# A two-product GELU kernel: another order for the opening loads and transposes, for the second block of b and for the late turns of a

## The chip, the cores and the metric

The kernel runs on one core of one Trainium2 chip. Times are device microseconds of one execution, lower is better. Profile times are microseconds from the start of the span unless marked ns.

## The reference

With a of 1024 x 1024, b of 1024 x 2048 and c of 2048 x 1024, all float32:

```python
h = np.matmul(a, b)
h = 0.5 * h * (1 + np.tanh(np.sqrt(2 / np.pi) * (h + 0.044715 * h ** 3)))
return np.matmul(h, c).astype(np.float32)
```

## The kernel before

The program is written with its order by hand: each engine executes its instructions in the order in which the kernel's lines issue them. PE is TensorE, DVE is VectorE, ACT is ScalarE, POOL is GpSimd, and SP is the queue that issues most loads and stores. POOL issues the loads that turn float32 into bf16 on the way.

The first product is made transposed: a block of 128 columns of b is the stationary operand, and 512 rows of a, transposed and in bf16, are the moving one. One result is therefore a tile of 128 columns of h by 512 rows, summed over eight slices of 128 along the contraction. There are 16 such tiles (t = 0 to 15) for each half of a's rows. ACT applies the GELU as it takes a tile out of PSUM. The transposes of a are made by PE, and DVE copies them out of PSUM.

The first half of a's rows goes in three stages:

- **Block one**, t = 0 to 5 (L102 for the products). SP loads a in five column groups across all four row tiles (L76, pieces of 512 or 1024 bytes) and eight slices of b, 768 columns wide (L82), alternately. For each slice k, DVE casts a's four blocks (L107), PE transposes them (L110), DVE copies them out (L111), ACT casts the slice of b in two halves (L113), and PE then multiplies the slice before. Ten products of zeros (L96) occupy PE at the head.
- **Block two**, t = 6 to 9 (L134). POOL loads its columns of b in four DMAs of two slices each (L126). The loop takes the slices outermost, so all four result tiles grow together in four PSUM buffers.
- **Tiles t = 10 to 15** (L143, in `mm1`), each of which takes all eight slices by itself. POOL loads their columns of b (`b_hi`) in four DMAs, and then the second half of a's rows in four DMAs of one row tile each (L155). `turn(j)` transposes one of these row tiles by eight transposes (L162) and one DVE copy (L163). The turns stand after t = 11, 12, 13 and 14.

POOL's loads of b start when a small copy on POOL, the gate (L91), has seen slice 5 of block one's b arrive. After the four turns the second half of a's rows goes through all 16 tiles.

The second product is a 2 x 2 block scheme with seven block products (L242), whose sums and differences of blocks DVE makes (L196 to L235). The sums of c begin when the second half-column of c has been loaded into the buffer that the transposed first half of a used. The last output tile is made in two pieces of 256 columns, each added (L312) and stored by itself.

PSUM is split into two pools: `ppool` with six buffers, and `tpool` with two, which the transposes use.

Of the kernel before, what the change touches and what calls it, by code (L numbers as in the profile page):

```python
# [9 lines left out]
F32 = mybir.dt.float32  # L10
BF16 = mybir.dt.bfloat16
F32R = mybir.dt.float32r
SUB = mybir.AluOpType.subtract
ADD = mybir.AluOpType.add
AF = mybir.ActivationFunctionType
# [4 lines left out]
def kernel(ctx, tc, a, b, c, out):  # L20
    nc = tc.nc
    M, K = a.shape
    _, N = b.shape
    _, P = c.shape
    KT = K // 128
    NT = N // 128
    MT = M // 128
    H = 512
    N0 = 6
    W0 = N0 * 128  # L30
    N1 = 4
    W1 = N1 * 128

    av = a.rearrange("(mt p) k -> p mt k", p=128)
# [6 lines left out]
    astage = ctx.enter_context(tc.tile_pool(name="astage", bufs=4))  # L41
    abf = ctx.enter_context(tc.tile_pool(name="abf", bufs=4))
# [3 lines left out]
    tpool = ctx.enter_context(tc.tile_pool(name="tpool", bufs=2, space=PSUM))  # L46

    warm = consts.tile([128, H], BF16, name="warm")
    nc.vector.memset(warm, 0.0)
    ident = consts.tile([128, 128], BF16, name="ident")  # L50
# [3 lines left out]
    aT = [keep.tile([128, KT, H], BF16, name=f"aT{h}", tag=f"A{h}") for h in range(2)]  # L54
    WB = W0 + W1
    b_lo = keep.tile([128, KT, WB], BF16, name="b_lo", tag="B0")
    b_hi = keep.tile([128, KT, N - WB], BF16, name="b_hi", tag="B1")

    def bcols(k0, kn, n0, w):
        if n0 < WB:  # L60
            return b_lo[:, k0:k0 + kn, ds(n0, w)]
        return b_hi[:, k0:k0 + kn, ds(n0 - WB, w)]

    def bt(k, t):
        return bcols(k, 1, t * 128, 128)[:, 0, :]
# [5 lines left out]

    a_st, b_st = {}, {}

    def load_a0(k, n):
        st = astage.tile([128, 4, 256], F32, name="a_st")
        nc.sync.dma_start(out=st[:, :, 0:n * 128], in_=av[:, 0:4, ds(k * 128, n * 128)])  # L76
        for i in range(n):
            a_st[k + i] = st[:, :, ts(i, 128)]

    def load_b0(k):  # L80
        st = b0stage.tile([128, W0], F32, name="b0_st")
        nc.sync.dma_start(out=st, in_=bv[:, k, 0:W0])  # L82
        b_st[k] = st

    gate = consts.tile([128, 1], F32, name="gate")
    for k, n in ((0, 1), (1, 1), (2, 2), (4, 2), (6, 2)):
        load_a0(k, n)
        for i in range(n):
            load_b0(k + i)

    nc.gpsimd.tensor_copy(gate, b_st[5][:, 0:1])  # L91
    g = consts.tile([128, 1], F32, name="g")
    nc.scalar.activation(g, warm[:, 0:1], AF.Gelu_apprx_tanh)
    wps = tpool.tile([128, H], F32, name="pt")
    for _ in range(10):
        nc.tensor.matmul(wps, warm[:, 0:128], warm, start=True, stop=True)  # L96

    ps = [ppool.tile([128, H], F32, name="ps") for _ in range(N0)]

    def mm0(k):  # L100
        for t in range(N0):
            nc.tensor.matmul(ps[t], bt(k, t), aT[0][:, k, :],  # L102
                             start=(k == 0), stop=(k == KT - 1))

    for k in range(KT):
        ab = abf.tile([128, 4, 128], BF16, name="ab")
        nc.vector.tensor_copy(ab, a_st[k])  # L107
        pt = tpool.tile([128, H], BF16, name="pt")
        for j in range(4):
            nc.tensor.transpose(pt[:, ts(j, 128)], ab[:, j, :], ident)  # L110
        nc.vector.tensor_copy(aT[0][:, k, :], pt)  # L111
        for i in range(2):
            nc.scalar.activation(b_lo[:, k, ts(i, W0 // 2)], b_st[k][:, ts(i, W0 // 2)], AF.Copy)  # L113
        if k > 0:
            mm0(k - 1)
    mm0(KT - 1)

    def gelu(t, h, p):
        nc.scalar.activation(hq[h][t // NH][:, t % NH, :], p, AF.Gelu_apprx_tanh)  # L119
# [5 lines left out]
    def load_b(k0, kn, n0, w):  # L125
        nc.gpsimd.dma_start(out=bcols(k0, kn, n0, w), in_=bv[:, k0:k0 + kn, ds(n0, w)])  # L126

    ps = [(tpool if t < 2 else ppool).tile([128, H], F32, name="pt" if t < 2 else "ps")
          for t in range(N1)]
    for k in range(0, KT, 2):  # L130
        load_b(k, 2, W0, W1)
        for i in range(2):
            for t in range(N1):
                nc.tensor.matmul(ps[t], bt(k + i, N0 + t), aT[0][:, k + i, :],  # L134
                                 start=(k + i == 0), stop=(k + i == KT - 1))
# [4 lines left out]
    def mm1(t, h):  # L140
        p = ppool.tile([128, H], F32, name="ps")
        for k in range(KT):
            nc.tensor.matmul(p, bt(k, t), aT[h][:, k, :],  # L143
                             start=(k == 0), stop=(k == KT - 1))
        gelu(t, h, p)
# [7 lines left out]
    for j in range(4):  # L153
        st = abf.tile([128, K], BF16, name="ab1")
# [3 lines left out]
    def turn(j):  # L158
        ab = a1[j]
        pt = tpool.tile([128, KT, 128], BF16, name="pt")  # L160
        for k in range(KT):
            nc.tensor.transpose(pt[:, k, :], ab[:, ts(k, 128)], ident)  # L162
        nc.vector.tensor_copy(aT[1][:, :, ts(j, 128)], pt)  # L163

    for t in range(N0 + N1, NT):
        mm1(t, 0)
        if NT - 5 <= t < NT - 1:
            turn(t - (NT - 5))

# [6 lines left out]
    c21 = keep.tile([128, NH, H], BF16, name="c21")  # L178
# [25 lines left out]
    for t in range(NT):  # L204
# [10 lines left out]
        if WB // 128 <= t < WB // 128 + 4:  # L215
            i = t - WB // 128
# [20 lines left out]
    def bank(w=H):  # L237
        return ppool.tile([128, w], F32, name="ps", padded_shape=[128, H])

    def prod(p, lhs, rhs, j, q=slice(0, H)):  # L240
        for t in range(NH):
            nc.tensor.matmul(p, lhs(t)[:, ts(j, 128)], rhs(t)[:, q],  # L242
                             start=(t == 0), stop=(t == NH - 1))

    def whole(x):
        return lambda t: x[:, t, :]
# [10 lines left out]
    def new_out():  # L257
        return opool.tile([128, H], F32, name="ot")

    def store(ot, m, q0, w=H):  # L260
        nc.sync.dma_start(out=out[ts(m, 128), ds(q0, w)], in_=ot[:, 0:w])

    def combine(m, q, p, u, op=ADD, swap=False):
        ot = new_out()
        nc.vector.tensor_tensor(ot, u if swap else p, p if swap else u, op=op)  # L265
        store(ot, m, q * H)
# [5 lines left out]
    for j in R:  # L272
        p = bank()
        prod(p, whole(h11), whole(c11), j)
        nc.scalar.activation(u2[j], p, AF.Copy)  # L275
    for j in range(3):
        p = bank()
# [3 lines left out]
    last_keep = opool.tile([128, H], F32, name="lk", bufs=1)  # L281
    nc.gpsimd.tensor_copy(last_keep, last)  # L282
    for j in R:
        p = bank()
        prod(p, halves(s2), ones(t2), j)
        nc.vector.tensor_tensor(u2[j], p, u2[j], op=ADD)
    for j in R:
        p = bank()
# [3 lines left out]
    for j in R:  # L292
        p = bank()
# [5 lines left out]
    for j in R:  # L299
        p = bank()  # L300
        prod(p, halves(s2), whole(c22), j)
        combine(j, 1, p, u2[j])
    for j in R:
        p = bank()
        prod(p, whole(h22), ones(t2), j)
        combine(4 + j, 0, p, u3[:, j, :], op=SUB, swap=True)
    for q in range(2):
        w = H // 2
        p = bank(w)
        prod(p, whole(h12), whole(c21), 3, q=ds(q * w, w))  # L310
        ot = new_out()
        nc.vector.tensor_tensor(ot[:, 0:w], p, last_keep[:, ds(q * w, w)], op=ADD)  # L312
        store(ot, 3, q * w, w)

# [1 line left out]
_INS = ['a', 'b', 'c']  # L316
# [26 lines left out]
```

## Time and profile before

| | |
|---|---|
| median of 13 runs | 126.71 us (125.42 to 127.51) |
| the profiled execution | 125.42 us, of which the span is 123.6 |
| PE | 114.5 us busy, 93% of the span |
| DVE | 65.2 us, 53% |
| ACT | 29.6 us, 24% |
| DMA | 18.43 MB written at their targets, 20.97 MB read from HBM |

A line of the timeline gives start, length, engine, source line, operation, operands and count, and in brackets the idle time just before it and what ended that. Matmuls are pipelined, so the starts of successive ones tell more than their lengths. A DMA's landing time is its issue's start plus its time to landing.

### The profile page before, as it was taken

How to read it: one execution, taken by the hardware profiler on the slowest of the kernel's cores; microseconds unless marked ns; L12 is line 12 of the kernel's file. 1: busy time of each engine (PE TensorE's matmuls, PEld its weight loads, DVE VectorE, ACT ScalarE, POOL GpSimd, SP SyncE). 2: the span in 40 equal slices, each digit the busy share in tenths (PEclk: the TensorE clock that was granted, in tenths of full speed). 3: DMA queues.
4: the chain of work that ended last, by engine and by line, in shares of the span. 5: the costliest groups of instructions: out<-in, count | busy, mean ns of one | idle time of the engine just before them, and what ended most of it. 6: DMA issues, size and time to landing. Idle time of an engine off the chain costs nothing.

```text
span 123.6 us, 1446 instructions
## 1 busy us (share of the span) xinstructions
PE 114.5 (93%) x562; PEld 66.9 (54%) x562; DVE 65.2 (53%) x94; ACT 29.6 (24%) x54; POOL 22.2 (18%) x28
## 2 busy tenths in 40 slices
PE   6947899999599999999999999999999999999990
PEld 2323344444255544444444444468888888888860
DVE  0134451000042200007999999999569999964440
ACT  4144456707211332333223332100000000000000
POOL 2000099433440130000000000895000000000000
PEclk9999999999999999999999999999999999999999
DMA  3799999999999999995000000001500022444433
GB/s 100 172 386 377 380 325 182 194 201 203 212 205 207 329 393 225 206 206 88 0 3 0 5 0 0 0 0 60 194 0 0 5 85 99 155 184 155 170 139 115
DMA packets 14245, 18.43 MB, mean 149 GB/s; under 512 B 800, under 2 KB 9760, under 8 KB 14240
## 3 DMA queue, kind: packets, MB, share of 16 engines
q0 software_dynamic: 8000, 8.91, 39.2%
q1 hardware_dynamic: 6240, 9.44, 21.6%
q8 instruction: 4, 0.07, 0.2%
q14 instruction: 1, 0.01, 0.0%
HBM read 20.97 MB, written 4.19 MB: 204 GB/s over the span
## 4 chain that ended last, share of the span: by engine, by line
PE 70%; DMA 17%; POOL 5%; SPq 4%; issue 0%; DVE 0%
PE ps L242 41%; PE ps L143 28%; DMA ab<-in_a_dram 10%; DMA b_st<-in_b_dram 7%; SPq L82 3%; POOL b_hi L126 2%; POOL b_lo L126 2%; SPq L76 2%; PE pt L162 2%; DVE ot L312 0%; POOL gate L91 0%
## 5 line engine op out<-in xcount | busy, mean ns | idle before, releaser
L119 ACT ACTIVATE h<-ps 128x512 fp32r<-128x512 f32 (+1 forms) x30 | 17.3, 601 | 28.6 <-PE ps L143 27.4
L143 PE MATMUL ps<-aT,b_hi 128*128 128x512 bf16 x96 | 21.7, 379 | 0.0
L143 PE MATMUL ps<-aT,b_lo 128*128 128x512 bf16 x80 | 17.4, 379 | 0.0
L242 PE MATMUL ps<-t,s 128*128 128x512 f32 x64 | 15.1, 393 | 0.0
L143 PEld LDWEIGHTS <-b_hi 128*128 128x128 bf16 x96 | 9.2, 98 | 10.4
L242 PE MATMUL ps<-t,h 128*128 128x512 f32 x64 | 14.8, 389 | 0.0
L242 PE MATMUL ps<-c,h 128*128 128x512 bf16 (+1 forms) x72 | 14.2, 356 | 0.0
L242 PEld LDWEIGHTS ps<-t,s 128*128 128x128 f32 x64 | 12.0, 188 | 2.6
L242 PEld LDWEIGHTS ps<-t,h 128*128 128x128 f32 x64 | 12.0, 188 | 2.5
L282 POOL COPY lk<-u 128x512 f32<-128x512 f32 x1 | 7.3, 7312 | 33.4 <-ACT u L275 33.4
L143 PEld LDWEIGHTS <-b_lo 128*128 128x128 bf16 x80 | 7.8, 98 | 9.5
L163 DVE COPY aT<-pt 128x1024 bf16<-128x1024 bf16 x4 | 2.8, 692 | 19.0 <-PE pt L162 19.0
L196 DVE TENSOR_TENSOR t<-c,c 128x1024 fp32r<-128x1024 bf16 x4 | 4.7, 1222 | 15.1 <-DMA c<-in_c_dram 14.9
L102 PE MATMUL ps<-aT,b_lo 128*128 128x512 bf16 x48 | 11.5, 379 | 0.0
L242 PEld LDWEIGHTS <-h 128*128 128x128 bf16 x72 | 7.0, 98 | 7.0 <-issue 0.3
L113 ACT ACTIVATE b_lo<-b_st 128x384 bf16<-128x384 f32 x16 | 7.5, 515 | 9.9 <-DMA b_st<-in_b_dram 9.8
L184 POOL DMA_DIRECT2D c<-in_c_dram x8 | 6.0, 745 | 13.1 <-PE ps L143 6.9
L265 DVE TENSOR_TENSOR ot<-ps,u 128x512 f32<-128x512 f32 x11 | 7.3, 683 | 1.1 <-PE ps L242 1.1
L242 PE MATMUL ps<-c,s 128*128 128x512 f32 x32 | 7.4, 389 | 0.0
L242 PEld LDWEIGHTS ps<-c,s 128*128 128x128 f32 x32 | 6.0, 188 | 1.2
L111 DVE COPY aT<-pt 128x512 bf16<-128x512 bf16 x8 | 3.4, 425 | 6.2 <-PE pt L110 6.2
L102 PEld LDWEIGHTS <-b_lo 128*128 128x128 bf16 x48 | 4.4, 98 | 4.0
(37 smaller groups left out, 92.6 us busy)
## 6 DMA issues: line engine op xcount, KB each, us to landing
out_dram<-ot SPq DMA_DIRECT2D x15, 256.0 KB, 2.1
b_st<-in_b_dram SPq DMA_DIRECT2D x8, 384.0 KB, 8.4
c<-in_c_dram POOLq DMA_DIRECT2D x6, 512.0 KB, 14.5
c<-in_c_dram POOLq DMA_DIRECT2D x2, 1024.0 KB, 15.4
a_st<-in_a_dram SPq DMA_DIRECT2D x3, 512.0 KB, 8.8
b_hi<-in_b_dram POOLq DMA_DIRECT2D x4, 384.0 KB, 9.9
b_lo<-in_b_dram POOLq DMA_DIRECT2D x4, 256.0 KB, 5.8
ab<-in_a_dram POOLq DMA_DIRECT2D x4, 256.0 KB, 12.7
```

What stands on the lines that cost most here:

```text
L82: nc.sync.dma_start(out=st, in_=bv[:, k, 0:W0])
L102: nc.tensor.matmul(ps[t], bt(k, t), aT[0][:, k, :], start=(k == 0), stop=(k == KT - 1))
L111: nc.vector.tensor_copy(aT[0][:, k, :], pt)
L113: nc.scalar.activation(b_lo[:, k, ts(i, W0 // 2)], b_st[k][:, ts(i, W0 // 2)], AF.Copy)
L119: nc.scalar.activation(hq[h][t // NH][:, t % NH, :], p, AF.Gelu_apprx_tanh)
L126: nc.gpsimd.dma_start(out=bcols(k0, kn, n0, w), in_=bv[:, k0:k0 + kn, ds(n0, w)])
L143: nc.tensor.matmul(p, bt(k, t), aT[h][:, k, :], start=(k == 0), stop=(k == KT - 1))
L184: nc.gpsimd.dma_start(out=dst[:, t:t + 4, :], in_=cv[:, r * NH + t:r * NH + t + 4, ts(q, H)])
L196: nc.vector.tensor_tensor(t1[i], c12[:, ts(i, 2), :], c11[:, ts(i, 2), :], op=SUB)
L242: nc.tensor.matmul(p, lhs(t)[:, ts(j, 128)], rhs(t)[:, q], start=(t == 0), stop=(t == NH - 1))
L265: nc.vector.tensor_tensor(ot, u if swap else p, p if swap else u, op=op)
L282: nc.gpsimd.tensor_copy(last_keep, last)
```

## The change

Four places are altered.

1. The opening. SP loads a by row tiles: tiles 0 and 1 in whole rows, tiles 2 and 3 as two half rows each, with the first two slices of b between the halves. The casts and transposes go by row tile and half row (four 128 x 128 blocks): `half` casts on DVE or on ACT, `turn0` transposes and copies out on DVE or on ACT. Six of the eight groups of transposes stand ahead of block one, and the second halves of tiles 2 and 3 inside its slices 1 and 2. Each slice of b is cast half on DVE and half on ACT. The products of zeros are eight at the head and three after the second and the fourth group; they write into the last of block one's PSUM buffers. The gate waits for slice 4 of b.
2. Block two's part of b comes in two DMAs of four slices.
3. The turns of the second half of a stand after t = 13 (one) and t = 14 (three).
4. The last output tile is cut into 384 and 128 columns.

```diff
-    def load_a0(k, n):
-        st = astage.tile([128, 4, 256], F32, name="a_st")
-        nc.sync.dma_start(out=st[:, :, 0:n * 128], in_=av[:, 0:4, ds(k * 128, n * 128)])
-        for i in range(n):
-            a_st[k + i] = st[:, :, ts(i, 128)]
+    def load_a0(mt, k0, n):
+        st = astage.tile([128, n * 128], F32, name="a_st")
+        nc.sync.dma_start(out=st, in_=av[:, mt, ds(k0 * 128, n * 128)])
+        a_st[mt, k0] = st
...
-    for k, n in ((0, 1), (1, 1), (2, 2), (4, 2), (6, 2)):
-        load_a0(k, n)
-        for i in range(n):
-            load_b0(k + i)
-
-    nc.gpsimd.tensor_copy(gate, b_st[5][:, 0:1])
+    load_a0(0, 0, KT)
+    load_a0(1, 0, KT)
+    load_a0(2, 0, 4)
+    load_a0(3, 0, 4)
+    load_b0(0)
+    load_b0(1)
+    load_a0(2, 4, 4)
+    load_a0(3, 4, 4)
+    for k in range(2, KT):
+        load_b0(k)
+
+    nc.gpsimd.tensor_copy(gate, b_st[4][:, 0:1])
...
-    wps = tpool.tile([128, H], F32, name="pt")
-    for _ in range(10):
-        nc.tensor.matmul(wps, warm[:, 0:128], warm, start=True, stop=True)
-
     ps = [ppool.tile([128, H], F32, name="ps") for _ in range(N0)]
 
-    def mm0(k):
+    def warm_up(n):
+        for _ in range(n):
+            nc.tensor.matmul(ps[N0 - 1], warm[:, 0:128], warm, start=True, stop=True)
+
+    warm_up(8)
+
+    def half(mt, k0, off=0):
+        src = a_st[mt, k0 - off][:, ds(off * 128, 512)]
+        ab = abf.tile([128, 512], BF16, name="ab")
+        if off or mt == 3:
+            nc.scalar.activation(ab, src, AF.Copy)
+        else:
+            nc.vector.tensor_copy(ab, src)
+        return ab
+
+    def turn0(mt, k0, ab):
+        pt = tpool.tile([128, 4, 128], BF16, name="pt")
+        for k in range(4):
+            nc.tensor.transpose(pt[:, k, :], ab[:, ts(k, 128)], ident)
+        dst = aT[0][:, k0:k0 + 4, ts(mt, 128)]
+        if k0 == 0 and mt != 2:
+            nc.vector.tensor_copy(dst, pt)
+        else:
+            nc.scalar.activation(dst, pt, AF.Copy)
+
+    HW = W0 // 2
+
+    def cast_b0(k):
+        nc.vector.tensor_copy(b_lo[:, k, 0:HW], b_st[k][:, 0:HW])
+        nc.scalar.activation(b_lo[:, k, HW:W0], b_st[k][:, HW:W0], AF.Copy)
+
+    steps = [(0, 0, 0), (0, 4, 4), (1, 0, 0), (1, 4, 4), (2, 0, 0), (3, 0, 0)]
+    ab = [half(*x) for x in steps[:2]]
+    for i, x in enumerate(steps):
+        if i % 2 == 0 and i + 2 < len(steps):
+            ab += [half(*y) for y in steps[i + 2:i + 4]]
+        turn0(x[0], x[1], ab[i])
+        if i in (1, 3):
+            warm_up(3)
+    cast_b0(0)
+    cast_b0(1)
+    for k in range(KT):
+        if k == 1:
+            ab = [half(2, 4), half(3, 4)]
+        if k > 0 and k + 1 < KT:
+            cast_b0(k + 1)
         for t in range(N0):
             nc.tensor.matmul(ps[t], bt(k, t), aT[0][:, k, :],
                              start=(k == 0), stop=(k == KT - 1))
+            if k in (1, 2) and t == 2:
+                turn0(k + 1, 4, ab[k - 1])
...
-    for k in range(0, KT, 2):
-        load_b(k, 2, W0, W1)
-        for i in range(2):
+    for k in range(0, KT, 4):
+        load_b(k, 4, W0, W1)
+        for i in range(4):
...
-        if NT - 5 <= t < NT - 1:
-            turn(t - (NT - 5))
+        if t == NT - 3:
+            turn(0)
+        if t == NT - 2:
+            turn(1)
+            turn(2)
+            turn(3)
...
-    for q in range(2):
-        w = H // 2
+    for q0, w in ((0, 384), (384, 128)):
         p = bank(w)
-        prod(p, whole(h12), whole(c21), 3, q=ds(q * w, w))
+        prod(p, whole(h12), whole(c21), 3, q=ds(q0, w))
```

The loop over the slices that stood here before (cast, four transposes, copy, two casts of b, products of the slice before) is taken out; it is in the kernel's code above.

More of the change, by code (lines that the diff above doesn't have):

```diff
@@ L103, in mm0 @@
                              start=(k == 0), stop=(k == KT - 1))
[L105 to L111, printed above, removed]
-        for i in range(2):
[L113 to L116, printed above, removed]
+            if k in (1, 2) and t == 2:
+                turn0(k + 1, 4, ab[k - 1])
     def gelu(t, h, p):
@@ L129 @@
           for t in range(N1)]
-    for k in range(0, KT, 2):
-        load_b(k, 2, W0, W1)
-        for i in range(2):
+    for k in range(0, KT, 4):
+        load_b(k, 4, W0, W1)
+        for i in range(4):
             for t in range(N1):
@@ L306 @@
         combine(4 + j, 0, p, u3[:, j, :], op=SUB, swap=True)
-    for q in range(2):
-        w = H // 2
+    for q0, w in ((0, 384), (384, 128)):
         p = bank(w)
-        prod(p, whole(h12), whole(c21), 3, q=ds(q * w, w))
+        prod(p, whole(h12), whole(c21), 3, q=ds(q0, w))
         ot = new_out()
-        nc.vector.tensor_tensor(ot[:, 0:w], p, last_keep[:, ds(q * w, w)], op=ADD)
-        store(ot, 3, q * w, w)
+        nc.vector.tensor_tensor(ot[:, 0:w], p, last_keep[:, ds(q0, w)], op=ADD)
+        store(ot, 3, q0, w)
 _INS = ['a', 'b', 'c']
```

## The prediction

> **What bounds the kernel now.** I read the page's busy shares first: PE 93% of 123.6 us, so only PE's gaps can be won. The PE timeline says where they are (start, length, engine and line, operation, count, idle before it and its releaser):
>
> ```profile
> 1.19 4.45 PE L96 MATMUL pt<-warm 128*128 128x512 bf16 x10 [1.19 <-DVE warm L49]
> 5.43 0.58 PE L110 MATMUL pt<-ident,ab 128*128 128x128 bf16 x4
> 7.84 0.40 PE L110 MATMUL pt<-ident,ab 128*128 128x128 bf16 x4 [1.82 <-DVE ab L107]
> 8.07 1.46 PE L102 MATMUL ps<-aT,b_lo 128*128 128x512 bf16 x6
> ...
> 19.09 2.75 PE L102 MATMUL ps<-aT,b_lo 128*128 128x512 bf16 x12
> 21.68 0.59 PE L134 MATMUL pt<-aT,b_lo 128*128 128x512 bf16 x2
> ...
> 28.58 3.62 PE L143 MATMUL ps<-aT,b_hi 128*128 128x512 bf16 x16
> 33.64 0.62 PE L162 MATMUL pt<-ident,ab 128*128 128x128 bf16 x8 [1.44 <-DMA ab<-in_a_dram]
> 34.10 1.89 PE L143 MATMUL ps<-aT,b_hi 128*128 128x512 bf16 x8
> ```
>
> The opening (block one, 48 products of L102) runs from 8.07 to 21.68, though twelve products take 21.68 - 19.09 = 2.59, or 0.216 each, so that 48 need 10.4. Block two (32 of L134) follows to 28.58 without a gap. Then one wait of 1.44 to 1.6 us, before the first turn (L162) at 33.64. The chain of waits confirms it, and shows nothing but PE after it:
>
> ```profile
> 21.37 12.22 DMA ab<-in_a_dram
> 33.59 0.05 issue
> 33.64 0.62 PE pt L162 x8
> ...
> 40.78 29.35 PE ps L143 x136
> 70.14 50.17 PE ps L242 x232
> ```
>
> The stage table (stretch, length, busy time of PE, PEld, DVE, ACT and POOL, clock, DMA share, GB/s) tells what feeds the opening:
>
> ```profile
> 3.00:4.00 1.00, 1.00 (x4) 0.33 (x3) 0.43 (x1) 0.00 (x0) 0.00 (x0) 1.00 1.13 221
> 4.00:5.00 1.00, 1.00 (x3) 0.30 (x2) 0.00 (x0) 0.00 (x0) 0.00 (x0) 1.00 0.54 124
> 5.00:6.00 1.00, 1.00 (x6) 0.52 (x4) 0.00 (x0) 0.13 (x1) 0.00 (x0) 1.00 0.47 140
> 6.00:7.00 1.00, 0.01 (x1) 0.00 (x0) 0.42 (x1) 0.81 (x2) 0.00 (x0) 1.00 1.10 387
> ```
>
> DMA is full from 6 us on at 370 to 390 GB/s, with a hole of about 1 us between 4 and 6. The same 5.24 MB are loaded after the change, so bytes in order decide.
>
> **What the Trainium skill says.** "DMA: Bandwidth & Descriptors", Queues, rings and completion order: an SDMA engine drains one queue's ring in order and alternates between queues. The trace agrees: a queue's landings come in issue order. "TensorE: Matmul & The Clock Gate", Part 1: the array starts at half clock and is released after a window of about 3.4 us of activity, which runs free of the kernel. The trace agrees: the ten warm-ups take 0.445 each, later products 0.216; four transposes take 0.58 at 5.43 and 0.40 at 7.84. "ScalarE: Activation LUTs", What ACT_TABLE_LOAD costs: an ACTIVATE is 186 ns + 0.833 per element, 612 for 512; the gelu row shows 594 to 606, and L113's 384 elements take 515 where the formula gives 506.
>
> **The change, part by part.**
>
> *1. Loads and start of block one.* SP issues 14 loads instead of 13 (0.43 to 0.5 each), a first. The first product now needs a's tiles 0, 1 and the halves of 2 and 3 (1.57 MB) and b's slice 0, and the next products slice 1: 2.36 MB. Before, issue plus time to landing in the tile view gives b slice 2 at 3.26 + 7.5 = 10.8 with 2.23 MB ahead of and in it, slice 3 at 3.81 + 8.0 = 11.8 with 2.62 MB. Interpolated, 2.36 MB is in at 11.1, and 1.57 MB (between slice 1, 1.31 MB at 8.3, and the third load of a, 1.84 MB at 9.8) at 9.05. The old order began with 0.52 MB of 512-byte packets; rows of 2 to 4 KB should be quicker. I take 0.45 off (estimate, between 0 and the hole's 1.0 more): halves of a at 8.6, slice 1 at 10.7. The two late halves of a wait on SP for a staging buffer, that is for the casts of tiles 0 and 1, with slices 2 to 7 behind them; the latter casts end near 8, when 0.8 MB or more is still queued, over 2 us, so DMA does not run dry.
>
> From 8.6 ACT has a cast (0.61), two copies from PSUM (0.61 each) and half a slice's cast (0.515): 10.95. DVE waits for the last transpose, which needs a PSUM buffer freed by ACT at 9.85: transposes 0.35, copy 0.43 (L111: 425 ns), half a slice 0.36 (from L107, 443 for 512): 11.0. Block one starts at **10.9** (9.7 to 11.7) instead of 8.07. It is then PE alone: 48 x 0.216 + two groups of four transposes at 0.23 = 10.8, end **21.75** instead of 21.68. Its casts keep up: slice k is due at 10.9 + 1.3k, and lands every 1.04 us (0.39 MB) from 10.7. The 24 other transposes (24 x 0.057 = 1.4) and the 6 added warm-ups (6 x 0.216 = 1.3) lie between 5 and 10.9, while PE waits for a; without that cover they would cost up to 2.7. ACT's total in the opening goes from 16 x 0.515 = 8.2 to 8 x 0.515 + 9 x 0.61 = 9.6, DVE's from 6.9 to about 5.9, both under 21.
>
> *2. Block two in two DMAs.* POOL issues 2 x 0.75 less, so the four b_hi loads and a's second half are queued 1.5 us earlier, behind full DMA engines: nothing won, and nothing lost, since POOL has only DMA issues until 77. The first product of block two now waits for four slices (1.05 MB read) rather than two. Before, the second of four loads landed at 16.2 + 5.5 = 21.7; the gate (slice 4 instead of 5) opens at 15.3 to 15.0 and less lies ahead, so 21.3 to 21.7, against PE at 21.75. I take 0, bounds 0 and 0.6; a win is excluded, since PE has no gap here now. The second half is due 3.45 later, at 25.2, where the last of the four landed at 24.35.
>
> *3. Late turns.* From block two's end E + 6.91 PE does four tiles (8 x 0.216 = 1.73 each), one turn (0.445), a tile, three turns, a tile. The first turn is due at 21.75 + 6.9 + 6.9 = 35.6; its tile landed at 33.6: the wait of 1.6 goes. The other three are due from 37.7; the last landed at 24.66 + 12.7 = 37.4. New: three turns in a row have two PSUM buffers, so the third waits for the first one's copy (L163, 0.69): 0.5. That copy pair at the end is hidden by the last tile's 1.73. Sum from the end of block one: 6.91 + 6 x 1.73 + 4 x 0.445 + 0.5 = 19.55, where it was 42.34 - 21.68 = 20.65 (1.6 of it waiting).
>
> *4. The end.* Two pieces of 256 columns become 384 and 128. PE: 8 x 0.16 + 8 x 0.057 (L162's pace) = 1.74 against 16 x 0.107 = 1.71. The last DVE addition shrinks from 0.42 to about 0.3, but waits for the bigger one before it (0.55). SP: two stores as before (0.33 each). I take 0, bounds -0.2 and +0.2.
>
> *Sum:* 21.75 + 19.55 = 41.3 against 42.34: **1.05 us** won. What follows must move up too:
>
> ```profile
> 56.40 2.36 DVE L196 TENSOR_TENSOR t<-c,c 128x1024 fp32r<-128x1024 bf16 x2 [14.89 <-DMA c<-in_c_dram]
> ...
> 75.41 4.62 DVE L226 TENSOR_TENSOR s<-s,h 128x1024 fp32r<-128x1024 f32 x4
> ...
> 87.74 0.69 DVE L286 TENSOR_TENSOR u<-ps,u 128x512 f32<-128x512 f32 x1 [0.18 <-PE ps L242]
> 89.63 0.69 DVE L286 TENSOR_TENSOR u<-ps,u 128x512 f32<-128x512 f32 x1 [1.19 <-PE ps L242]
> ```
>
> DVE waits for c at 56.4, which a full DMA brings no sooner, and is then behind until 87.7. Its sums s2 are done at 80.0, PE wants them at 81.9: 1.85 us of slack, so 1.05 passes through and little over 1.9 would.
>
> The profiled execution took 125.42 (span 123.6 and 1.8 around it), the lowest of 13 with median 126.71. 125.42 - 1.05 = 124.37, 0.992 of it; on the median, **125.7**.
>
> **Rivals.**
> *Hole gone.* The 1 us hole may belong to the 512-byte packets and the hop between tensors. Then loads come 1 us earlier, block one starts near 9.7, and 1.9 is won before the s2 slack is used up: 124.8. Against it: the first 512-byte packets moved 281 GB/s before the hole, so it may lie in the memory and stay.
> *Late start eats it.* No packet gain, or a link more in the ACT and DVE chain: block one at 11.7, end 22.5, 0.3 won: 126.4. For it: ACT carries four 0.6 us steps in series just there.
> *Half clock (slower).* Before, ten warm-ups in one piece made PE busy from 1.19 to 5.64. Now eight end near 4.6, and bursts of 0.4 to 1.3 us with gaps up to 2 us follow until 10.9. If the activity window falls badly, block one begins at 0.427 per product. A window of 3.4 us costs 1.7, the 4.2 us or more seen at the start (1.19 to past 5.43) 2.1; from 2.1 us at half speed on the gain is gone. That gives 127.4 to 127.8. For it: the window is free; against it: before, gaps of 1.8 with single transposes between them did no harm.
> That the late turns do not do what they say, because a's second half lands late again, would give back up to 1.6 and falls under the second rival.
>
> **How the numbers follow.** 0.50 for the forecast (its own range 125.0 to 126.05), 0.15 hole gone, 0.17 late start, 0.18 half clock. 0.5% is 0.63 us, about what a measurement here can tell from no change. Faster 0.50 + 0.15 = 0.65, same 0.17, slower 0.18. The range takes in the hole's case with its bounds below and most of half clock: 124.0 to 127.6.
>
> **What would show it.** First L148 product at 10.9 and 48 of them without a wait; block two within 0.6 after; no wait of a turn for DMA, but 0.5 before the fourth; start of the second half's tiles at 41.3; everything after it 1.05 earlier, with no PE wait at s2. Wrong if products of block one are spaced 0.427, if ACT or DVE casts hold PE inside it, if the hole has another length, or if the first s2 product waits for DVE.

## The result and the profile after

| | before | after |
|---|---|---|
| median of all runs | 126.93 us (48) | 124.01 us (11) |
| lowest to highest | 125.36 to 129.16 | 123.53 to 125.58 |
| profiled execution (span) | 125.42 (123.6) | 123.99 (122.2) |

The ratio of after to before is 0.982, with a 95% interval of 0.979 to 0.986: faster by 1.8%, some 2.3 us. The two profiled executions differ by only 1.43 us. The ratio compares fast executions alone (up to 1.5% above the fastest of their kernel), so it lies nearer 1 than the quotient of the medians does. Each execution has a recorded mean TensorE clock; "at full clock" below means that it is 0.99 or more.

The PE timeline of the changed kernel (start, length, engine and line, operation, count, idle before it and its releaser):

```profile
1.19 3.60 PE L103 MATMUL ps<-warm 128*128 128x512 bf16 x8 [1.19 <-DVE warm L49]
...
7.64 0.39 PE L119 MATMUL pt<-ident,ab 128*128 128x128 bf16 x4
8.49 0.38 PE L119 MATMUL pt<-ident,ab 128*128 128x128 bf16 x4 [0.46 <-ACT aT L124]
9.66 2.26 PE L148 MATMUL ps<-aT,b_lo 128*128 128x512 bf16 x9 [0.79 <-DVE b_lo L129]
11.91 0.40 PE L119 MATMUL pt<-ident,ab 128*128 128x128 bf16 x4
12.14 0.81 PE L148 MATMUL ps<-aT,b_lo 128*128 128x512 bf16 x3
13.42 0.82 PE L148 MATMUL ps<-aT,b_lo 128*128 128x512 bf16 x3 [0.47 <-DVE b_lo L129]
...
14.30 7.29 PE L148 MATMUL ps<-aT,b_lo 128*128 128x512 bf16 x33
21.43 0.59 PE L169 MATMUL pt<-aT,b_lo 128*128 128x512 bf16 x2
...
28.33 7.07 PE L178 MATMUL ps<-aT,b_hi 128*128 128x512 bf16 x32
35.24 0.61 PE L197 MATMUL pt<-ident,ab 128*128 128x128 bf16 x8
35.69 1.89 PE L178 MATMUL ps<-aT,b_hi 128*128 128x512 bf16 x8
37.41 1.06 PE L197 MATMUL pt<-ident,ab 128*128 128x128 bf16 x16
38.80 0.61 PE L197 MATMUL pt<-ident,ab 128*128 128x128 bf16 x8 [0.33 <-DVE aT L198]
39.25 1.89 PE L178 MATMUL ps<-aT,b_hi 128*128 128x512 bf16 x8
40.97 5.34 PE L178 MATMUL ps<-aT,b_lo 128*128 128x512 bf16 x24
```

Block one (L148) now runs from 9.66 to 21.43, where it ran from 8.07 to 21.68. The wait of a turn for DMA is gone; in its place stands the 0.33 us before the fourth turn. The second half of a's rows starts at 40.97 instead of 42.34, and that 1.37 us reaches the end whole. The chain of waits says the same: after block one it has PE and one 0.7 us copy, and ahead of that the loads of b's slice 2.

```profile
6.40 6.58 DMA b_st<-in_b_dram
...
13.42 0.82 PE ps L148 x3
...
38.06 0.70 DVE aT L198
...
39.41 29.35 PE ps L178 x136
68.76 49.71 PE ps L281 x224
```

The stage table of the opening (stretch, length, busy time of PE, PEld, DVE, ACT and POOL, clock, DMA share, GB/s):

```profile
3.00:4.00 1.00, 1.00 (x4) 0.33 (x3) 0.00 (x0) 0.00 (x0) 0.00 (x0) 1.00 1.00 389
4.00:5.00 1.00, 1.00 (x6) 0.38 (x5) 0.43 (x1) 0.63 (x1) 0.00 (x0) 1.00 1.01 350
...
8.00:10.00 2.00, 0.76 (x7) 0.52 (x7) 0.69 (x2) 1.42 (x3) 0.00 (x0) 1.00 0.85 245
10.00:12.00 2.00, 2.00 (x11) 0.60 (x9) 0.79 (x2) 0.52 (x1) 0.00 (x0) 1.00 1.04 409
```

The hole at 4 to 6 us is gone, and a slow stretch stands at 8 to 10, when slices 0 and 1 of b arrive.

### The profile page after: what moved, and what is told of

Its sections match the earlier page's. It is cut to its first block, busy times and chain, and to the rows that moved or that the text cites. A ratio compares the mean times of both kernels' runs of the same rounds, so it can differ in the third digit from the quotient of the medians.

```text
span 122.2 us, 1452 instructions
## 1 busy us (share of the span) xinstructions
PE 115.7 (95%) x566; PEld 67.3 (55%) x566; DVE 64.0 (52%) x93; ACT 31.2 (26%) x55; POOL 21.9 (18%) x26
## 4 chain that ended last, share of the span: by engine, by line
PE 85%; DMA 9%; DVE 1%; issue 1%; SPq 1%; ACT 1%; DVEq 0%
PE ps L281 41%; PE ps L178 31%; PE ps L148 7%; DMA b_st<-in_b_dram 5%; DMA a_st<-in_a_dram 3%; PE ps L169 3%; PE pt L169 3%; PE pt L197 1%; SPq L76 1%; DVE aT L198 1%; ACT ab L111 1%; DVE b_lo L129 0%; DVEq L376 0%; PE pt L119 0%; DVE ot L350 0%
## 5 line engine op out<-in xcount | busy, mean ns | idle before, releaser
L178 PEld LDWEIGHTS <-b_hi 128*128 128x128 bf16 x96 | 9.3, 98 | 10.8
L281 PE MATMUL ps<-c,h 128*128 128x512 bf16 (+2 forms) x72 | 14.2, 355 | 0.0
L321 POOL COPY lk<-u 128x512 f32<-128x512 f32 x1 | 8.1, 8083 | 33.2 <-ACT u L314 33.2
L148 PE MATMUL ps<-aT,b_lo 128*128 128x512 bf16 x48 | 11.2, 380 | 1.3 <-DVE b_lo L129 1.3
L148 PEld LDWEIGHTS <-b_lo 128*128 128x128 bf16 x48 | 4.4, 98 | 6.9 <-DVE b_lo L129 2.4
L103 PE MATMUL ps<-warm 128*128 128x512 bf16 x14 | 5.7, 560 | 1.2 <-DVE warm L49 1.2
L129 DVE CAST b_lo<-b_st 128x384 bf16<-128x384 f32 x8 | 3.0, 369 | 5.2 <-DMA b_st<-in_b_dram 5.2
```

Source lines behind the costliest of these rows:

```text
L103: nc.tensor.matmul(ps[N0 - 1], warm[:, 0:128], warm, start=True, stop=True)
L129: nc.vector.tensor_copy(b_lo[:, k, 0:HW], b_st[k][:, 0:HW])
L148: nc.tensor.matmul(ps[t], bt(k, t), aT[0][:, k, :], start=(k == 0), stop=(k == KT - 1))
L178: nc.tensor.matmul(p, bt(k, t), aT[h][:, k, :], start=(k == 0), stop=(k == KT - 1))
L281: nc.tensor.matmul(p, lhs(t)[:, ts(j, 128)], rhs(t)[:, q], start=(t == 0), stop=(t == NH - 1))
```

## The experiments

The ratios are to the kernel before, each on the chip of its own batch.

| run | what it is | median us | ratio, 95% interval |
|---|---|---|---|
| e1 | before, late turns alone | 124.54 | 0.987 (0.981 to 0.993) |
| e2 | before, opening alone | 126.19 | 0.996 (0.992 to 0.999) |
| e3 | before, two DMAs for block two alone | 125.82 | 0.997 (0.994 to 0.999) |
| e4 | the changed kernel, same chip | 124.77 | 0.985 (0.979 to 0.990) |

The kernel before had a median of 127.12 there. The first theory (A) gave the gain to the late turns, the rival (B) to the opening.

### e1: the late turns alone

```diff
-        if NT - 5 <= t < NT - 1:
-            turn(t - (NT - 5))
+        if t == NT - 3:
+            turn(0)
+        if t == NT - 2:
+            turn(1)
+            turn(2)
+            turn(3)
```

> The kernel before with the late turns alone. Theory A (the gain is the wait for a's second half, 1.6 us, less 0.5 for the third and fourth turn sharing two PSUM buffers): block one still starts near 8.1 and ends near 21.7, the second half's tiles start at block one's end + 19.55 (before 20.65), so 1.1 us faster than before. Theory B (the opening carries the gain, the wait would have moved or come back elsewhere): at most 0.3 us faster, with a new wait of a turn for DMA.

It is 1.7 us faster, most of the whole gain, so A holds against B; but it is more than the 1.1 that A gave. In its profile the second half starts 41.48 - 21.93 = 19.55 after the end of block one, just as A has it. Its PE timeline (the lines before the last) and POOL timeline (last line) show where the rest can come from:

```profile
28.83 7.07 PE L143 MATMUL ps<-aT,b_hi 128*128 128x512 bf16 x31
35.74 0.61 PE L162 MATMUL pt<-ident,ab 128*128 128x128 bf16 x8
...
39.30 0.61 PE L162 MATMUL pt<-ident,ab 128*128 128x128 bf16 x8 [0.34 <-DVE aT L163]
...
41.48 3.83 PE L143 MATMUL ps<-aT,b_lo 128*128 128x512 bf16 x17
...
34.78 0.74 POOL L188 DMA_DIRECT2D c<-in_c_dram x1 [0.52 <-DMA ab<-in_a_dram]
```

POOL's fifth load of c waits for the first tile of a's second half, and so dates its landing. It is released at 34.78 here, 0.9 us later than in the profiled execution of before (33.88). The turn does not notice, since it is due at 35.74. In the old place it would have cost 0.9 us more (an estimate: 34.78 - 33.88).

### e2: the opening alone

Loads, casts, transposes, warm-ups and gate of the changed kernel, everything after it as before.

> The kernel before with the new opening alone (loads, casts, transposes, warm-ups and gate); four DMAs of two slices for block two, turns after t = 11 to 14, equal end pieces. Theory A: block one ends up to 0.3 us earlier, and the wait at the first turn grows by as much, since a's second half lands at 33.3 to 33.6 as before: within 0.3 us of before. Theory B: 1 us or more faster than before, because the loads as a whole (and with them a's second half) come sooner.

It is 0.5 us faster (0.1 to 1.0), between A and B, and neither is shown by it. Block one ended some 0.5 us sooner, and the wait at the first turn grew from 1.44 to 2.16:

```profile
28.08 3.62 PE L178 MATMUL ps<-aT,b_hi 128*128 128x512 bf16 x16
33.86 0.62 PE L197 MATMUL pt<-ident,ab 128*128 128x128 bf16 x8 [2.16 <-DMA ab<-in_a_dram]
```

The first turn's tile decides when this wait ends, not PE. What is won probably comes from that landing. The load of c that it releases goes out at 34.10 here, and at 33.1 to 34.0 in seven other profiles with the new loads (the changed kernel, e4, e6, e7, e9, e11 and e12). With the old loads it goes out at 34.59 to 35.10 in e1, e3, e5 and e8, and at 33.88 in the profile of the kernel before. So the new loads probably bring a's second half some 0.5 to 1.0 us sooner than is usual before.

### e3: block two's part of b in two DMAs, alone

```diff
-    for k in range(0, KT, 2):
-        load_b(k, 2, W0, W1)
-        for i in range(2):
+    for k in range(0, KT, 4):
+        load_b(k, 4, W0, W1)
+        for i in range(4):
```

> The kernel before with block two's part of b in two DMAs of four slices, nothing else. Theory A: the first product of block two waits 0 to 0.6 us for four slices that land at 21.4 to 21.9 instead of two; the turn's wait for a takes that back, so within 0.3 us of before. Theory B's rival for this part (fewer DMAs bring a's second half earlier): a's first tile lands 0.7 us or more before 33.6 and the kernel is as much faster.

The wait came, 0.24 us before block two, and it was 0.4 us faster all the same (0.1 to 0.8), just over A's 0.3. a's first tile did not land sooner: the release of c is at 34.59. Why the change gains at all is not settled. None of its 20 executions has a mean clock of 0.973, against 13 of 41 of the kernel before on the same chip, though its first turn still waits 1.64 us.

### e4: the changed kernel on the same chip, and the clock

> The changed kernel again, on the same chip as the three parts. Theory A: 1.4 us faster than before where the granted clock is full in both, and the sum of the three parts' gains is within 0.4 of it. If the 2.2 us of the medians is real and not from slower chips among the runs of before, it shows here too, and the runs of before must have a cost that its profiled execution does not have (a longer turn wait, or a clock below 1.0 at the start).

It is 1.9 us faster at the ratio, and the three parts sum to 2.7 us. Opening and turns act on the same wait, so they may overlap; the intervals of the runs are too wide to show it. The profiled execution took 125.32 and is the half-clock rival of the prediction. Its stage table (the clock is the third column from the right), and the PE timeline's line of block one's start:

```profile
7.70:11.10 3.40, 1.63 (x12) 1.01 (x13) 1.03 (x4) 2.12 (x5) 0.00 (x0) 0.99 0.93 296
11.10:14.50 3.40, 3.18 (x11) 1.49 (x11) 1.23 (x4) 2.13 (x5) 0.00 (x0) 0.51 1.04 416
14.50:17.90 3.40, 3.40 (x20) 1.69 (x19) 1.35 (x4) 2.45 (x6) 2.53 (x4) 1.00 0.93 287
```

```profile
10.24 3.30 PE L148 MATMUL ps<-aT,b_lo 128*128 128x512 bf16 x9 [0.79 <-DVE b_lo L129]
```

PE was busy for 1.63 of 3.40 us, with no gap over 0.8, and the next 3.4 us ran at half clock: nine products in 3.30 instead of 2.12 to 2.26. The second half starts at 42.28, 1.3 us later than at full clock. Over three batches 7 of 24 executions of the changed kernel have a mean clock of 0.985 or 0.986, and take 125.2 to 125.8; the other 17 take 123.5 to 124.9.

### e5 and e8: what the wait before the first turn does to the clock

The kernel before has 78 executions in all batches with a recorded clock. 37 are at full clock (125.2 to 127.5, median 126.4), and 20 at 0.973, two stretches of half clock, with 127.6 to 129.1. Theory C laid the second stretch to the wait before the first turn; theory D to the opening or to DMA. One run filled the wait with work, another lengthened it:

```diff
+        if t == NT - 5:
+            wz = ppool.tile([128, H], F32, name="ps")
+            for _ in range(6):
+                nc.tensor.matmul(wz, warm[:, 0:128], warm, start=True, stop=True)
         if NT - 5 <= t < NT - 1:
             turn(t - (NT - 5))
```

> The kernel before with six more products of zeros just ahead of its first turn (6 x 0.216 = 1.3 us of PE work inside the wait of 1.4 to 1.6 us); turns, loads and all else as before. Theory C (the wait before the first turn costs twice: itself, and in about half of the executions a stretch of TensorE at half clock after it): the full-clock executions stay at 125.4 to 126.5, the executions at 127.5 to 129 with mean clock 0.973 go, and the median falls by 0.8 to 1.5 us. Theory D (the spread of the kernel before comes from its opening or from DMA, and the wait is only a wait): median and spread as before, or 0.1 to 0.3 us slower.

```diff
-        if NT - 5 <= t < NT - 1:
-            turn(t - (NT - 5))
+        if NT - 6 <= t < NT - 2:
+            turn(t - (NT - 6))
```

> The kernel before with its turns one tile earlier (after t = 10 to 13), so that PE waits some 3.3 us instead of 1.5 for a's second half; the tile that stood before the wait now comes after it. Theory C: the clock column falls to about 0.5 for 3.4 us or more after the wait, and the execution is 1.7 us (the moved tile) plus 1.7 us or more slower than before: 128.8 to 130.5. Theory D: clock stays 1.0 and it is 1.7 us slower, 127.1 to 127.6.

e8 took 129.68. Its PE timeline, and its stage table around the wait:

```profile
34.48 0.76 PE L162 MATMUL pt<-ident,ab 128*128 128x128 bf16 x8 [3.86 <-DMA ab<-in_a_dram]
35.03 3.48 PE L143 MATMUL ps<-aT,b_hi 128*128 128x512 bf16 x8
38.35 0.61 PE L162 MATMUL pt<-ident,ab 128*128 128x128 bf16 x8
```

```profile
31.50:34.90 3.40, 0.42 (x7) 0.42 (x8) 0.00 (x0) 0.00 (x0) 1.66 (x3) 0.99 1.16 209
34.90:38.30 3.40, 3.40 (x12) 1.34 (x10) 0.69 (x1) 0.00 (x0) 1.30 (x2) 0.51 1.16 207
```

After the wait the clock is 0.51 for 3.4 us, and eight products take 3.48 us instead of 1.89: the wait is paid twice. The clock row of e8's page (40 slices of 3.2 us, tenths of full speed) shows this stretch and an earlier one in the opening:

```profile
PEclk9967999999959999999999999999999999999998
```

Two such stretches make 0.973 of a mean (2 x 3.4 x 0.5 of 126). In e5 none of 14 executions is at 0.973 (4 of 19 of the kernel before on that chip), and the highest is 127.51. Its median fell by 0.45, less than C's 0.8; by the ratio nothing is won (0.9995, 0.996 to 1.004), since the wait for DMA itself stays.

So e8 shows C for a wait of 3.86 us. That the wait of some 1.5 us does it in the kernel before is likely and not shown: no execution of it at 0.973 was profiled, e3 has none at 0.973 with the wait in place, and e1 has one of six (and two at 0.981 and 0.982) with the wait gone.

The recorded clock also misses something. The profile of e5 has a mean clock of 1.0, and yet its first twelve products of block one are some 0.42 apart, as at half clock. Up to there e5 does not differ from the kernel before. The PE timeline, and a stretch of the stage table:

```profile
8.40 2.77 PE L102 MATMUL ps<-aT,b_lo 128*128 128x512 bf16 x6
10.96 0.63 PE L110 MATMUL pt<-ident,ab 128*128 128x128 bf16 x4
11.39 2.70 PE L102 MATMUL ps<-aT,b_lo 128*128 128x512 bf16 x6
```

```profile
8.40:10.90 2.50, 2.50 (x8) 0.91 (x7) 0.85 (x2) 0.94 (x2) 0.00 (x0) 1.00 1.05 395
```

Block one ends at 22.81 there instead of 21.68. Counts of half clock by this record are therefore lower bounds: an execution "at full clock" can have a slow opening.

### e6: the opening's gaps filled

```diff
         if i in (1, 3):
             warm_up(3)
+        if i == 4:
+            warm_up(2)
+        if i == 5:
+            warm_up(4)
```

> The changed kernel with six more products of zeros in the gaps of its opening: two after the fifth group of transposes and four after the sixth. Theory C (the changed kernel's slower executions, clock 0.986, are half clock at the start of block one, because PE was less than half busy in the window before): no execution at 0.986 with 125.2 to 125.7, all within 123.5 to 124.5. Theory D (the 0.986 has another cause): a third of the executions stay at 125.2 to 125.7. If the added products delay the transposes, 0.1 to 0.3 us slower throughout.

All six executions have a mean clock of 0.996 or more; five take 123.65 to 124.36, and one 125.74. With e11, which has the same products, that is none of 12 at 0.986, against 7 of 24 of the changed kernel. But one execution of each (125.74 and 125.21) is as slow as those at 0.986 are, and what slowed them is not known. So it is likely, and not shown, that filling the gaps rids the kernel of the executions of 125.2 and more. The ratio (0.983, 0.977 to 0.990) is no better than the changed kernel's.

### e7, e9 and e10: the slow stretch at 8 to 10 us

e7 loads the late halves of a into a buffer of their own:

```diff
-    load_a0(2, 4, 4)
-    load_a0(3, 4, 4)
+    load_late(2)
+    load_late(3)
```

> The changed kernel with the two late halves of a loaded into a buffer of their own, so that SP does not wait with them and with slices 2 to 7 of b for the casts of tiles 0 and 1. Theory E (the slow stretch at 8 to 10 us is the memory answering slowly on b's first slices): the late loads are issued by 4.5, but slice 2 still lands at 12.5 to 13.2 and block one ends within 0.2 us of 21.4. Theory F (DMA runs dry because SP waits): no slow stretch, slice 2 lands by 12.2, block one ends 0.5 to 0.9 us sooner, and the kernel gains that.

SP's and PE's timeline and the stage table:

```profile
3.54 0.94 SPq L89 DMA_DIRECT2D late<-in_a_dram x2
4.52 6.42 SPq L81 DMA_DIRECT2D b_st<-in_b_dram x6
```

```profile
13.38 0.82 PE L155 MATMUL ps<-aT,b_lo 128*128 128x512 bf16 x3 [0.48 <-DVE b_lo L136]
```

```profile
8.00:9.00 1.00, 0.31 (x4) 0.30 (x4) 0.00 (x0) 1.00 (x3) 0.00 (x0) 1.00 0.59 184
```

The loads go out by 4.5, and yet DMA is 0.59 busy at 184 GB/s, and PE waits for slice 2 at the same place. Theory F (SP starves the queue) falls. The kernel's time did not change (123.94 and 124.02 at full clock; the other two of its four executions, at 0.986, took 125.55 and 125.64).

e9 puts a small load of b's slices first, and e10 puts the two slices themselves first:

```diff
+    feel = consts.tile([128, 2, 16], F32, name="feel")
+    nc.sync.dma_start(out=feel, in_=bv[:, 0:2, 0:16])
     load_a0(0, 0, KT)
```

> The changed kernel with one small load put first: 64 bytes of each of the 256 rows of b's slices 0 and 1, which nothing reads. Theory G (the slow stretch at 8 to 10 us is the first access to b's rows, and a small access pays it as well as a large one): DMA at 8 to 10 us runs at 380 GB/s or more instead of 190 to 340, slice 2 lands by 12.3 instead of 13.0, and block one ends 0.4 to 0.9 us sooner, less about 0.5 for the load itself. Theory H (the slow stretch belongs to moving these slices, whatever came before): rates at 8 to 10 us as before, and the kernel is 0 to 0.6 us slower.

> The changed kernel with slices 0 and 1 of b ahead of all loads of a. Theories G and H: the slow stretch moves with b to 3 to 6 us, and a's tiles are loaded at 340 GB/s or more after it; block one starts within 0.5 us of 10. A rate set by the time since the start or by the change from a to b: the first slices of b land by 4.5 at full rate, and a slow stretch comes later, at a or at slice 2.

The stage tables of e9 (two lines) and of e10 (three lines):

```profile
2.00:3.00 1.00, 1.00 (x4) 0.42 (x3) 0.00 (x0) 0.22 (x2) 0.00 (x0) 1.00 0.87 90
...
8.00:9.00 1.00, 1.00 (x10) 0.54 (x8) 0.26 (x1) 0.99 (x2) 0.00 (x0) 1.00 0.91 294
```

```profile
3.00:4.00 1.00, 1.00 (x4) 0.32 (x3) 0.00 (x0) 0.00 (x0) 0.00 (x0) 1.00 1.13 246
4.00:5.00 1.00, 0.73 (x2) 0.00 (x0) 0.00 (x0) 0.00 (x0) 0.00 (x0) 1.00 0.74 152
...
6.00:7.00 1.00, 0.00 (x0) 0.00 (x0) 0.00 (x0) 0.00 (x0) 0.00 (x0) 1.00 1.02 418
```

In e10 the slow stretch moves with the slices to 3 to 5 us, and a then loads at 418. So, in this one execution, it belongs to b's first slices, not to the time since the start. In e9 the rate at 8 to 9 is higher, but the start now has 90 GB/s, and nothing is won (124.23, ratio 0.981, 0.973 to 0.988). That a small access pays the cost ahead is therefore not shown, and what makes the first slices slow stays open. e10 as a whole took 126.66. Block one started at 13.25, and not near 10: a's first transposes began at 8.06, and the clock was at half from 8 to 11.4 while they ran. Slices 2 to 7, which SP held until 9.9 behind the late halves, made the gate late as well (17.16 instead of 15.01).

### e11 and e12: slice 2 ahead of the late halves

e11 has e6's products as well:

```diff
-    load_a0(2, 4, 4)
-    load_a0(3, 4, 4)
-    for k in range(2, KT):
+    load_b0(2)
+    load_a0(2, 4, 4)
+    load_a0(3, 4, 4)
+    for k in range(3, KT):
```

> The changed kernel with the six further products of zeros in its opening's gaps, and with slice 2 of b loaded ahead of the two late halves of a (their casts and transposes one slice later). Theory I (block one of the changed kernel is held by slice 2 alone, behind the late halves): slice 2 lands 1.0 to 1.4 us sooner, block one has no wait of more than 0.2 us inside and ends near 20.6; block two then waits 0 to 0.5 us for its first four slices; 0.4 to 0.7 us faster than the changed kernel at full clock, and no execution near 0.986. Rival: the late halves become what is waited for, at slice 4, and nothing is won.

> The changed kernel once more, beside the one above on the same chip: at full clock 123.6 to 124.7, and about a third of its executions at mean clock 0.986 with 125.2 to 125.7.

Slice 2 is cast at 11.85 instead of 13.38, and block one waits 0.26 us inside (10.31 to 21.40, less 10.83 of work) where the changed kernel beside it waits 0.43 (10.54 to 21.80). So slice 2 did hold block one, but not alone and not by as much as theory I has it: what is won inside is 0.2 us and not 0.9, since block one starts at 10.3 and not at 9.7, nearer to the time when slice 2 lands. On the chip the two are the same: ratios 0.979 (0.974 to 0.985) and 0.979 (0.973 to 0.985), medians 123.91 and 124.20. No version here is shown to beat the changed kernel; e6 and e11 only lack, in 12 executions, those at 0.986.

## Why the prediction was right or wrong

Faster was right. That 124.01 lies in the range is luck, since the lower edge is 124.0 and was drawn for the rival with the hole gone: the forecast of 1.05 us was less than half of what came.

**Late turns: right.** From block one's end to the second half: 19.55 forecast, 40.97 - 21.43 = 19.54 measured. The wait that takes the place of the old one was sized 0.5 and is 0.33.

**Opening: the end right, its parts not.** Block one ends at 21.43 (forecast 21.75), but only because two errors cancel. It starts at 9.66 instead of 10.9 (at 9.9 to 10.5 in e2, e4, e6, e7, e9 and e12, so the profiled execution is an early one), because tiles 0 to 3 meet no hole and the halves of tiles 2 and 3 landed at 1.64 + 4.8 = 6.4 and 2.11 + 5.1 = 7.2, not 8.6. It then lasts 11.77 instead of 10.8. The failed step is "lands every 1.04 us from 10.7": slice 1 did land at 3.06 + 7.6 = 10.7, but the two late halves, 0.52 MB or some 1.3 us at 400 GB/s, come between it and slice 2, and were left out. Slice 2 lands at 6.40 + 6.6 = 13.0, and from a start at 9.66 it is due at 12.5 (twelve products and one group of transposes). Its wait is 0.63 of the 0.94 us that block one lasts too long; the rest is slice 1 and the first late half, whose transposes wait for a cast at 11.42. With slice 2 ahead of the late halves (e11) it is cast 1.5 us sooner and its wait is gone. The "hole gone" rival was half right: gone for a, and moved to b's first slices. e7 shows that it is not SP's waiting, and e10 that it is not the time since the start; its cause stays open.

**Two DMAs: right here.** The first four slices landed at 15.33 + 5.6 = 20.9, ahead of PE at 21.43. Alone (e3) they made PE wait 0.24, and in e9, where block one ends as late, 0.84, over the bound of 0.6. "A win is excluded" was wrong for e3, which was 0.4 us faster for a reason that stays open.

**The end: right.** From the first of the last products to the end of the span, 5.2 us before (123.6 - 118.37) and 5.2 after (122.2 - 116.98). The last addition takes 0.28 instead of 0.42.

**What follows: right.** DVE got c at 55.84 and had s2 done at 79.4, PE wanted it at 80.5: no wait, though 1.1 us of slack is left of the 1.85.

```profile
55.84 2.36 DVE L235 TENSOR_TENSOR t<-c,c 128x1024 fp32r<-128x1024 bf16 x2 [15.70 <-DMA c<-in_c_dram]
...
74.81 4.62 DVE L265 TENSOR_TENSOR s<-s,h 128x1024 fp32r<-128x1024 f32 x4
```

**The term that was mis-sized** is the wait for a's second half, taken as 1.6 us from one execution, which the text itself called the lowest of 13. The step "125.42 - 1.05, on the median 125.7" carried that execution's wait over to the median. In e1, e3, e5 and e8, which have the old loads, the tile's landing, dated by POOL, is 0.7 to 1.2 us later than in it, and the late turns take that up too: the turn of e1 was due at 35.74 and its tile was there by 34.78. At full clock the median of before is 126.4 and of after 124.0: 2.4 us, of which 1.43 is the difference of the profiled pair, and about 1.0 is how far the profiled execution of before lies under its own median. The later landings are of that size; since only one execution of before was profiled, that they are the cause is argued from the other four.

**Half clock** was named as the rival that ends slower, and it does happen, in 7 of 24 executions; but it cost 1.3 us in e4, less than the 1.7 to 2.1 priced, probably since the stretch also covers time that block one would have spent waiting for slice 2, and it stood against a gain of more than twice the forecast. The argument against this rival, that the gaps of before "did no harm", held for its profiled execution alone: in e5 and e8 the same opening ran at half pace. It was overlooked that the kernel before pays too: 20 of its 78 executions have a mean clock worth two such stretches, one of which, going by e8, may follow the wait at the turn.

## What to carry to other kernels

A wait at the edge of its slack is not one number: before you size what its removal brings, ask how much the landing behind it varies, and whether the profiled execution is a lucky one. Move the consumer to where its due time exceeds the latest landing seen, rather than the mean. Price a PE gap with what it does to the clock afterwards: a stretch of 3.4 us in which PE is less than half busy can be paid a second time, though it need not be.

## What the runs showed of the hardware

- The Trainium skill, "TensorE: Matmul & The Clock Gate", Part 1, has the half clock return after an idle window of about 3.4 us. Here it returned after a stretch of 3.40 us with PE busy for 1.63 and no gap over 0.8 (e4); in the changed kernel's own profile a stretch with 2.17 of 3.41 busy kept full clock. The busy share alone does not decide: in the profile of before a stretch with 1.58 of 3.40 busy (4.6 to 8.0, second line) kept full clock.

```profile
6.35:9.76 3.41, 2.17 (x22) 1.44 (x21) 1.54 (x4) 2.24 (x5) 0.00 (x0) 1.00 0.95 275
...
4.60:8.00 3.40, 1.58 (x10) 0.82 (x9) 0.85 (x2) 0.94 (x2) 0.00 (x0) 1.00 0.79 271
```

- The recorded clock can read 1.0 while products are at half pace: twelve of them some 0.42 us apart in e5, and the first products of zeros at the head, which are as far apart in every profile.
- The first slices of b loaded slowly wherever they stood (124 to 140 GB/s before at 4 to 6 us, 245 after at 8 to 10, 152 in e10 at 4 to 5), and later slices at 370 or more until POOL's loads begin.
